# A hybrid RWKV-7 / gated DeltaNet layer on one core: the woven order set anew, and three lists of products cut differently

## The chip, the cores and the metric

The kernel runs on one core of a Trainium2 chip. A core has TensorE (PE in the profile, with its weight loads as PEld), VectorE (DVE), ScalarE (ACT), GpSimd (POOL) and SyncE (SP), which issues most DMA transfers. The metric is the device time of one execution in microseconds (us); lower is better.

## What is computed

One layer over 256 latent and 256 context tokens, model width 2048, in fp32. Cut to what matters:

```python
mod = silu(c) @ w_ada + b_ada                  # first 4096 columns: shift and scale of norm 1
h, hc = modulate(rmsnorm(x)), modulate(rmsnorm(ctx))
rw, cv, z, ab, gt = split(h @ w_in)            # the same for hc
# RWKV-7: 16 heads of 64, both directions, context states start the latent scan
s = s * w_t - (s @ kk_t) b_t + v_t k_t         # per token; run here in chunks of 64
# gated DeltaNet: 8 heads of 128, both directions, chunks of 64
lmat = strict((k * beta) @ k.T * decay)        # solved by a triangular inverse
v_new = u_i - w_i @ s                          # the first chunk's state is zero
s = s * gl_i + k_tail_i.T @ v_new              # the state after the last chunk is not read
y = (sigmoid(g_a) * (o_a @ p_a) + sigmoid(g_b) * (o_b @ p_b)) @ w_out
x = x + gt1 * y
x = x + gt2 * swiglu(modulate(rmsnorm(x)))
return rmsnorm(x)
```

The kernel handles the DeltaNet in blocks of 128 tokens: four blocks, two of context and two of latent tokens, `gorder[d]` is the order in which direction d walks over them. The state product `NW` (L1411 to L1416) belongs to blocks 2 to 4 of that order, the state update (`kta`) to blocks 1 to 3.

## The kernel before

**Matrix products.** Weights come as fp32 and are split into two parts, `whi` (rounded, by ScalarE) and `wlo` (the rest, by VectorE); three TensorE products hi x hi, hi x lo, lo x hi replace one in fp32. These are the gemm products below (`mm<-hxh,whi` and so on). All other products run in plain fp32 and show as two records each in a trace.

**Start (L422 to L546).** A matvec makes shift and scale of the first norm. It runs in eight parts (`NE`), each with 64 products `mm<-aw,ckr` of 128 columns in tiles of 32 output rows. The weights of a part come in four loads `aw` of 1 MB (`load_ada`), and two loads `w_low` (`load_low`) bring the low-rank and first head weights of the same part. `ada_part(ps, e, c)` does a quarter of a part, `low_products` gives six tiles of gemm products of the part before, and `TILES[part][c]` says how many of those tiles stand behind visit c. `rows_of` turns the result of a part and normalises its share of the tokens; tiles that are left go there.

**The woven stage (L1506 to L1526).** RWKV pairs of heads, DeltaNet heads, the input projection (`products`), its casts (`cast`), the low-rank outputs and the second matvec (`ada_rest`) are written as generators. `Weave` takes one step of one of them after another. It keeps an estimated time for each engine, starts the step that can start first, and breaks ties by `RANK` (lower first). A step that reads what another engine made is placed `LAT['hop']` later, a change of the kind of TensorE product costs `LAT['turn']`, a load costs its bytes plus `LAT['dma']`. The order that results is fixed in the program, and each engine works its own queue in that order. TensorE fills the time between the small products of a chain with gemm products.

```python
at = w[3] + (0.0 if w[4] is None else lane.own if w[4] is lane else HOP)
key = (max(self.free.get(lane, 0.0), at), w[0])
```

**What a pair of RWKV heads does.** `prepare`, then `grams` (products `pa<-LAc` and `pa<-LAl`, once a direction), then `inverse`, `values` and `scan`. `invert` writes the blocks out to memory (`scr`), reads them back as 16x16 blocks, solves those on VectorE, writes them out (`tscr`) and reads them again. Then come lists of small TensorE products with one bank of PSUM (`pib`): a first list on 32x32 tiles, a second one with `Tx`, a third and a fourth. RWKV inverts 16 blocks at a time (`nu == 16`), a DeltaNet head 8.

**Low-rank outputs (`lowrank`).** Four loads of `lora` weights (one for two pairs) go through the same SP queue as everything else; each feeds eight products `s<-lin,wraw`.

**The merge stage (from L1563)** is scheduled by the compiler's own scheduler, and some of its first instructions come to stand among the last of the woven stage: casts of `rows` to `oah`, casts of weights (L370), sigmoids of the gates (`gts`).

Of the kernel before, what the change touches and what calls it, by code (L numbers as in the profile page):

```python
# [11 lines left out]
F32 = mybir.dt.float32  # L12
F32R = mybir.dt.float32r
AF = mybir.ActivationFunctionType
# [4 lines left out]
P = 128  # L19
# [7 lines left out]
DECAY = 0.6065306597126334  # L27
GATES_A, GATES_B = (6, 2, 3, 3, 0, 1, 4, 3), (2, 2, 0, 1, 0, 2, 10, 1)

RANK = dict(cast=-94, lowrank=60, prepare=59, grams=34, inverse=-56, values=6, scan=-39, begin=196, head_scan=145, head_inverse=100, head_grams=123, decays=137, tokens=77, features=120, gate_out=137, lowrank_out=105, row_tile=486)  # L30
LAT = dict(dma=2.04, hop=0.255, own=0.092, grp=32, cg=4, turn=0.17)
LNEXP = "natural_log_exp_and_others"
SIGM = "sigmoid_and_others"
UNIT = 64 * 64 + 64
# [249 lines left out]
def emit(ctx: ExitStack, tc, A, out, dbg=None):  # L284
# [6 lines left out]
    e, v, s = Lane(E, 0.0, 0.0, 0.0), Lane(V, 0.07, 0.00104, LAT["own"], 0.13), Lane(S, 0.09, 0.00086, LAT["own"], 0.165)  # L291
# [130 lines left out]
    with tc.tile_pool(name="p0", bufs=1) as p0, \  # L422
# [12 lines left out]
        def load_ada(e, c):  # L435
            w = aws[e, c] = p0.tile([P, 4, 4, P], F32, tag="aw", name="aw", bufs=6)
            Q.dma_start(w, A["ada_first"][e, :, 4 * c:4 * c + 4])
# [16 lines left out]
        ps = pst(pa, "pa")  # L454
# [9 lines left out]
        ps = pst(pa, "pa")  # L464
# [48 lines left out]
        def low_products(e, w):  # L513

            for ps, (o, m, n) in zip(low, LOWS):
                for k in range(2):
# [1 line left out]
                         e == 0 and k == 0, e == NE - 1 and k == 1)  # L518
                yield

        TILES = ((0, 0, 0, 0), (1, 1, 1, 1), (1, 1, 1, 1), (0, 2, 1, 1), (0, 1, 2, 1),
                 (0, 2, 1, 1), (0, 1, 2, 1), (0, 1, 1, 1), (0, 2, 1, 1))
        before = None
        for part in range(NE + 1):
            if part < NE:
                ps = pst(pmm, "mm")
            for c in range(4):
                if part + 1 < NE:
                    load_ada(part + 1, c)
                if part < NE:  # L530
                    ada_part(ps, part, c)
                if c == 0 and part < NE:
                    w = low_split(part)
                    if part + 1 < NE:
                        load_low(part + 1)
                for _ in itertools.islice(before or (), TILES[part][c]):
                    pass
            if part < NE:
                rows_of(part, ps, before or ())
                before = low_products(part, w)  # L540
            else:
                for _ in before:
                    pass
# [31 lines left out]
    def invert(pool, Lt, parts, nu, which, full, fill):  # L575
# [56 lines left out]
        ps = yield pib  # L632
# [3 lines left out]
        for d in range(2):  # L636
            yield v.scalar_tensor_tensor(Qm[:, us[d]], pv[:, 0, us[d]], low16[:, d:d + 1],
                                         eye16[:, d].unsqueeze(1).to_broadcast([P, h2, 16]), ALU.mult, ALU.add)
        if nu == 16:
            yield [e.matmul(pv[64 * h:64 * h + 64, 1, u], Tx[64 * h:64 * h + 64, u, :], Qm[64 * h:64 * h + 64, u, :],  # L640
                            start=True, stop=True) for u in range(nu) for h in range(2)]
        else:
            yield [e.matmul(pv[r, 1, u], Tx[r, u, b:b + 32], Qm[r, u, :], start=True, stop=True) for h, u, b, r in fours]
        for h in range(2):
            yield [(s.copy if h else v.tensor_copy)(T0[r, us[d], b + 16 * d:b + 16 * d + 16], pv[r, 1, us[d]])
                   for d in range(2) for b in (0, 32) for r in (slice(64 * h + b, 64 * h + b + 32),)]
# [641 lines left out]
    def tokens(h):  # L1288

        o = hd[h]  # L1290
        yield "feat", h
        yield "scan", NPAIR - 1 if h else NPAIR - 2
        yield "inverse", NPAIR - 1
        if h > 1:
            yield "gscan", h - 2
        o["keg"] = keg = gs.tile([P, 2, 4, P], F32, tag="keg", name="keg")
        o["kta"] = kta = gs.tile([P, 2, 4, P], F32, tag="kta", name="kta")
        o["vt"] = vt = gs.tile([P, 4, P], F32, tag="vt", name="gvt")
        ps = yield pab
        yield [e.transpose(ps[:, P * b:P * b + P], o["v"][:, P * b:P * b + P], ident) for b in range(4)]  # L1300
        yield s.copy(vt.rearrange("p b c -> p (b c)"), ps)
        weave.release(pab)
        ps = yield pab
        yield [e.transpose(ps[:, P * b:P * b + P], o["k"][:, P * b:P * b + P], ident) for b in range(4)]
        p4 = ps.rearrange("p (b c) -> p b c", b=4)
        for d in range(2):
            col = 8 * d + h
            yield v.tensor_mul(keg[:, d], p4, egc[:, :, col:col + 1].to_broadcast([P, 4, P]))
            yield v.tensor_mul(kta[:, d], p4, eta[:, :, col:col + 1].to_broadcast([P, 4, P]))
        weave.release(pab)  # L1310
        weave.ready("tok", h)

# [87 lines left out]
    def head_scan(h):  # L1400
# [7 lines left out]
            yield "out", NPAIR - 1  # L1408
        tf, keg, kta, vt, Qe, PT = (o[n] for n in ("tf", "keg", "kta", "vt", "Qe", "PT"))

        NW = gs.tile([P, 2, 4, P], F32, tag="NW", name="NW")  # L1411
        for d in range(2):
            ps = yield psb
            yield [e.matmul(ps[:, P * b:P * b + P], keg[:, d, b, :], tf[:, 4 * d + b, :], start=True, stop=True) for b in range(4)]
            yield s.activation(NW[:, d].rearrange("p b c -> p (b c)"), ps, AF.Identity, scale=-1.0)
            weave.release(psb)  # L1416
        if h:
            yield "gout", h - 1
# [2 lines left out]
        for n in range(4):  # L1421
            bs = (gorder[0][n], gorder[1][n])
            ps = yield psb
            yield [e.matmul(ps[:, P * d:P * d + P], tf[:, 4 * d + bs[d], :], vt[:, bs[d], :], start=True, stop=n == 0) if i == 0 else
                   e.matmul(ps[:, P * d:P * d + P], NW[:, d, bs[d], :], St[:, d, :], start=False, stop=True)
                   for d in range(2) for i in range(1 + (n > 0))]
            Vn = gs.tile([P, 2, P], F32, tag="Vn", name="Vn")
            for d in range(2):
# [383 lines left out]
```

## Time and profile before

| | |
|---|---|
| median of 3 runs | 2216.26 us (2205.15 to 2219.96) |
| the profiled execution | 2212.82 us, span 2211.0 us |
| mean granted TensorE clock | 0.989 |
| TensorE busy | 2138.1 us, 97% |
| VectorE, ScalarE, GpSimd busy | 1560.2 us, 1081.2 us, 93.6 us |
| read from and written to memory | 405.76 MB, 25.84 MB |

The span reaches from the first to the last instruction; some 2 us lie around it. Line numbers in a profile are those of the kernel; where the weave issues an instruction, its line is L147, and tiles tell such groups apart. Tiles that lie in one large buffer all show as `arena`. A row like `pi<-arena,Tx 64*64 64x16` is a product into a bank `pi`, 64 rows by 64 columns of the array, with 16 columns streamed. Busy TensorE time counts products that overlap in the array once.

### The profile page before, as it was taken

What the parts mean: (1) busy time and instruction counts of PE and PEld (TensorE: products, weight loads), DVE (VectorE), ACT (ScalarE), POOL (GpSimd) and SP (SyncE); (2) the same over time, 40 slices, a digit from 0 to 9 for tenths busy, and PEclk for the clock granted to TensorE, in tenths of its full rate; (3) what the DMA queues carried; (4) which work ended last, traced back from release to release, by engine and by line L of the source; (5) the groups of instructions that cost most, each with busy time, mean ns of one, the idle gap of its engine ahead of it and who ended that gap; (6) DMA issues with size and microseconds to landing.
All of it is one profiled execution on the core that took longest, in us unless ns stands there. A gap on an engine that the chain in (4) does not pass through costs nothing. (4 is left out here: it accounts for less than half of the span.)

```text
span 2211.0 us, 54434 instructions
## 1 busy us (share of the span) xinstructions
PE 2138.1 (97%) x22780; PEld 1910.8 (86%) x22780; DVE 1560.2 (71%) x3245; ACT 1081.2 (49%) x1915; POOL 93.6 (4%) x171
## 2 busy tenths in 40 slices
PE   6998999999999999999899899999999999999998
PEld 4776678787788788887789799999999999999997
DVE  3456788888798577998998689956665655444444
ACT  3248745545456555454554465534444444444443
POOL 0000000000000010111110010100000000000000
PEclk9999899999999999999999999999999999999999
DMA  9966544444444355565567888927777776566665
GB/s 383 413 188 201 152 117 108 120 109 109 121 113 112 111 182 167 177 195 167 170 202 251 291 297 303 344 78 236 237 235 233 230 234 198 186 184 187 188 185 160
DMA packets 234486, 435.13 MB, mean 197 GB/s; under 512 B 115329, under 2 KB 129665, under 8 KB 229889
## 3 DMA queue, kind: packets, MB, share of 16 engines
q1 hardware_dynamic: 206304, 355.11, 51.1%
q0 software_dynamic: 14112, 51.39, 7.1%
q10 hardware_dynamic: 13824, 25.17, 3.4%
q8 instruction: 178, 2.92, 0.6%
q14 instruction: 68, 0.55, 0.1%
HBM read 405.76 MB, written 25.84 MB: 195 GB/s over the span
## 5 line engine op out<-in xcount | busy, mean ns | idle before, releaser
L371 DVE TENSOR_TENSOR wlo<-wraw,whi 128x1024 fp32r<-128x1024 f32 x328 | 392.7, 1198 | 319.5 <-ACT whi L370 317.4
L370 ACT CAST whi<-wraw 128x1024 fp32r<-128x1024 f32 x328 | 337.9, 1031 | 461.3 <-PE mm L381 410.6
L147 PE MATMUL mm<-hxh,wlo 128*128 128x256 f32 (+1 forms) x1376 | 460.6, 335 | 5.7 <-DVE wlo L147 5.5
L147 PE MATMUL mm<-hxh,whi 128*128 128x256 f32 (+1 forms) x1376 | 461.9, 336 | 0.9 <-ACT arena L147 0.5
L147 PE MATMUL mm<-hxl,whi 128*128 128x256 f32 (+1 forms) x1376 | 460.8, 335 | 0.0
L380 PE MATMUL mm<-hfh,whi 128*128 128x256 f32 x1344 | 376.8, 280 | 0.0
L381 PE MATMUL mm<-hfl,whi 128*128 128x256 f32 x1344 | 375.8, 280 | 0.0
L382 PE MATMUL mm<-hfh,wlo 128*128 128x256 f32 x1344 | 374.6, 279 | 0.1
L147 PEld LDWEIGHTS mm<-hxh,wlo 128*128 128x128 f32 x1376 | 260.1, 189 | 33.6 <-DVE wlo L147 8.4
L147 PEld LDWEIGHTS mm<-hxh,whi 128*128 128x128 f32 x1376 | 260.1, 189 | 27.1 <-issue 4.4
L147 PEld LDWEIGHTS mm<-hxl,whi 128*128 128x128 f32 x1376 | 260.2, 189 | 26.1 <-issue 6.2
L147 DVE TENSOR_TENSOR wlo<-wraw,whi 128x512 fp32r<-128x512 f32 x344 | 236.9, 691 | 49.5 <-ACT whi L147 48.0
L382 PEld LDWEIGHTS mm<-hfh,wlo 128*128 128x128 f32 x1344 | 252.6, 188 | 0.6 <-DVE wlo L371 0.5
L381 PEld LDWEIGHTS mm<-hfl,whi 128*128 128x128 f32 x1344 | 252.7, 188 | 0.0
L380 PEld LDWEIGHTS mm<-hfh,whi 128*128 128x128 f32 x1344 | 252.5, 188 | 0.0
L147 ACT CAST whi<-wraw 128x512 fp32r<-128x512 f32 x344 | 205.2, 616 | 96.2 <-PE mm L147 63.4
L147 DVE TENSOR_TENSOR arena<-arena 128x28 f32<-128x28 f32 (+13 forms) x538 | 132.1, 247 | 18.7 <-DMA arena<-scr 7.1
L380 PE MATMUL mm<-za,whi 128*128 128x256 f32 x512 | 144.0, 281 | 0.0
L381 PE MATMUL mm<-za,whi 128*128 128x256 f32 x512 | 143.3, 280 | 0.0
L382 PE MATMUL mm<-za,wlo 128*128 128x256 f32 x512 | 142.4, 278 | 0.0
L147 ACT ACTIVATE arena<-arena 128x512 f32<-128x512 f32 (+3 forms) x132 | 76.8, 592 | 40.1 <-DVE arena L147 37.3
L381 PEld LDWEIGHTS mm<-za,whi 128*128 128x128 f32 x512 | 96.3, 188 | 0.0
(329 smaller groups left out, 3911.3 us busy)
## 6 DMA issues: line engine op xcount, KB each, us to landing
wraw<-w SPq DMA_DIRECT2D x172, 512.0 KB, 4.3
wraw<-wgu SPq DMA_DIRECT2D x168, 512.0 KB, 4.7
aw<-ada_rest POOLq DMA_DIRECT2D x96, 512.0 KB, 5.5
aw<-ada_first SPq DMA_DIRECT2D x32, 1024.0 KB, 12.6
wraw<-wdn SPq DMA_DIRECT2D x64, 448.0 KB, 3.6
wraw<-wout SPq DMA_DIRECT2D x32, 512.0 KB, 6.3
aw<-ada_gt ACTq DMA_DIRECT2D x64, 256.0 KB, 4.9
wraw<-wdn SPq DMA_DIRECT2D x32, 512.0 KB, 3.6
```

What stands on the lines that cost most here:

```text
L147: return Op(self, cost, lambda: getattr(self.engine, name)(out, *a, **k), kind)
L370: S.copy(hi[:, c, :M], raw[:, c, :M])
L371: V.tensor_sub(lo[:, c, :M], raw[:, c, :M], hi[:, c, :M].bitcast(F32))
L380: E.matmul(ps, hi, Xh[:, k, :n], start=first and i == 0, stop=False)
L381: E.matmul(ps, hi, Xl[:, k, :n], start=False, stop=False)
L382: E.matmul(ps, lo, Xh[:, k, :n], start=False, stop=last and i == len(wt) - 1)
```

## The change

It has four parts.

- `RANK` and two of the estimates in `LAT` get other numbers: a hand-over between engines (`hop`) 0.2167 instead of 0.255 us, a change of kind (`turn`) 0.1819 instead of 0.17.
- The start takes two quarters of a part in one visit, and their loads are issued together.
- With 16 blocks, `invert` builds its second list from 64 products on 32x32 tiles, as it does with 8 blocks; before it had 32 products on 64x64 tiles.
- `NW` has three blocks a direction instead of four, without the first of the order; in the second direction `keg` of the first block and `kta` of the last are not made either.

```diff
-RANK = dict(cast=-94, lowrank=60, prepare=59, grams=34, inverse=-56, values=6, scan=-39, begin=196, head_scan=145, head_inverse=100, head_grams=123, decays=137, tokens=77, features=120, gate_out=137, lowrank_out=105, row_tile=486)
-LAT = dict(dma=2.04, hop=0.255, own=0.092, grp=32, cg=4, turn=0.17)
+RANK = dict(cast=-94, lowrank=43, prepare=59, grams=36, inverse=-56, values=6, scan=-66, begin=196, head_scan=150, head_inverse=132, head_grams=123, decays=125, tokens=77, features=120, gate_out=97, lowrank_out=105, row_tile=486)
+LAT = dict(dma=2.04, hop=0.2167, own=0.092, grp=32, cg=4, turn=0.1819)
...
-        TILES = ((0, 0, 0, 0), (1, 1, 1, 1), (1, 1, 1, 1), (0, 2, 1, 1), (0, 1, 2, 1),
-                 (0, 2, 1, 1), (0, 1, 2, 1), (0, 1, 1, 1), (0, 2, 1, 1))
+        TILES = ((0, 0), (2, 2), (2, 2), (2, 2), (1, 3), (2, 2), (1, 3), (1, 2), (2, 2))
         before = None
         for part in range(NE + 1):
             if part < NE:
                 ps = pst(pmm, "mm")
-            for c in range(4):
+            for c in range(2):
                 if part + 1 < NE:
-                    load_ada(part + 1, c)
+                    for i in (2 * c, 2 * c + 1):
+                        load_ada(part + 1, i)
                 if part < NE:
-                    ada_part(ps, part, c)
+                    for i in (2 * c, 2 * c + 1):
+                        ada_part(ps, part, i)
                 if c == 0 and part < NE:
                     w = low_split(part)
                     if part + 1 < NE:
...
         for d in range(2):
             yield v.scalar_tensor_tensor(Qm[:, us[d]], pv[:, 0, us[d]], low16[:, d:d + 1],
                                          eye16[:, d].unsqueeze(1).to_broadcast([P, h2, 16]), ALU.mult, ALU.add)
-        if nu == 16:
-            yield [e.matmul(pv[64 * h:64 * h + 64, 1, u], Tx[64 * h:64 * h + 64, u, :], Qm[64 * h:64 * h + 64, u, :],
-                            start=True, stop=True) for u in range(nu) for h in range(2)]
-        else:
-            yield [e.matmul(pv[r, 1, u], Tx[r, u, b:b + 32], Qm[r, u, :], start=True, stop=True) for h, u, b, r in fours]
+        yield [e.matmul(pv[r, 1, u], Tx[r, u, b:b + 32], Qm[r, u, :], start=True, stop=True) for h, u, b, r in fours]
         for h in range(2):
             yield [(s.copy if h else v.tensor_copy)(T0[r, us[d], b + 16 * d:b + 16 * d + 16], pv[r, 1, us[d]])
                    for d in range(2) for b in (0, 32) for r in (slice(64 * h + b, 64 * h + b + 32),)]
...
         p4 = ps.rearrange("p (b c) -> p b c", b=4)
         for d in range(2):
             col = 8 * d + h
-            yield v.tensor_mul(keg[:, d], p4, egc[:, :, col:col + 1].to_broadcast([P, 4, P]))
-            yield v.tensor_mul(kta[:, d], p4, eta[:, :, col:col + 1].to_broadcast([P, 4, P]))
+            late, soon = (slice(0, 4 - d), slice(d, 4))
+            yield v.tensor_mul(keg[:, d, late], p4[:, late], egc[:, late, col:col + 1].to_broadcast([P, 4 - d, P]))
+            yield v.tensor_mul(kta[:, d, soon], p4[:, soon], eta[:, soon, col:col + 1].to_broadcast([P, 4 - d, P]))
         weave.release(pab)
         weave.ready("tok", h)
 
...
             yield "out", NPAIR - 1
         tf, keg, kta, vt, Qe, PT = (o[n] for n in ("tf", "keg", "kta", "vt", "Qe", "PT"))
 
-        NW = gs.tile([P, 2, 4, P], F32, tag="NW", name="NW")
+        NW = gs.tile([P, 2, 3, P], F32, tag="NW", name="NW")
         for d in range(2):
             ps = yield psb
-            yield [e.matmul(ps[:, P * b:P * b + P], keg[:, d, b, :], tf[:, 4 * d + b, :], start=True, stop=True) for b in range(4)]
-            yield s.activation(NW[:, d].rearrange("p b c -> p (b c)"), ps, AF.Identity, scale=-1.0)
+            yield [e.matmul(ps[:, P * i:P * i + P], keg[:, d, b, :], tf[:, 4 * d + b, :], start=True, stop=True)
+                   for i, b in enumerate(gorder[d][1:])]
+            yield s.activation(NW[:, d].rearrange("p b c -> p (b c)"), ps[:, :3 * P], AF.Identity, scale=-1.0)
             weave.release(psb)
         if h:
             yield "gout", h - 1
...
             bs = (gorder[0][n], gorder[1][n])
             ps = yield psb
             yield [e.matmul(ps[:, P * d:P * d + P], tf[:, 4 * d + bs[d], :], vt[:, bs[d], :], start=True, stop=n == 0) if i == 0 else
-                   e.matmul(ps[:, P * d:P * d + P], NW[:, d, bs[d], :], St[:, d, :], start=False, stop=True)
+                   e.matmul(ps[:, P * d:P * d + P], NW[:, d, n - 1, :], St[:, d, :], start=False, stop=True)
                    for d in range(2) for i in range(1 + (n > 0))]
             Vn = gs.tile([P, 2, P], F32, tag="Vn", name="Vn")
             for d in range(2):
```

Where the order of the program changes, at three places. First TensorE in the start, part 1 of the matvec (a piece of the difference; `aw,ckr` are the matvec's products, `C,rows` turns part 0, `hxh,whi` and `hxl,whi` begin the first low-rank tile).

```order
 L483 MATMUL pa<-C,rows 128x128
-L475 MATMUL mm<-aw,ckr 32x128 x16
+L475 MATMUL mm<-aw,ckr 32x128 x32
 L380 MATMUL pi<-hxh,whi 128x512
 L381 MATMUL pi<-hxl,whi 128x512
```

A visit that had a quarter of the part now has half of it. Over the whole start TensorE goes to the matvec 15 times instead of 24.

Second the queue of SyncE around the first inversion and the fourth load of low-rank weights, before and then now (`scr` is the list being written and read, `tscr` the solved blocks, `w` weights of the input projection, `sgd` low-rank outputs read back, `gts` a stored gate).

```order
L169 DMA scr_105<-arena 64x8x64 x3
L169 DMA wraw<-w 128x1024 x2
L169 DMA scr_105<-arena 64x8x64
L169 DMA arena<-sgd__1347 128x512
L169 DMA wraw<-lora 96x1024
L169 DMA arena<-scr_105 128x16x16
L169 DMA wraw<-w 128x1024 x2
```

```order
L169 DMA wraw<-w 128x1024 x2
L169 DMA scr_105<-arena 64x8x64 x3
L1062 DMA gts__1356<-arena 128x256
L169 DMA wraw<-w 128x1024
L169 DMA scr_105<-arena 64x8x64
L169 DMA arena<-sgd__1347 128x512
L169 DMA wraw<-lora 96x1024
L169 DMA arena<-scr_105 128x16x16
L169 DMA wraw<-w 128x1024 x2
```

The load of `lora` still stands behind the fourth piece of `scr` and one of `sgd`. Between the third and the fourth piece there is now one load of `w` and a stored gate where two loads of `w` were. On TensorE there stand, between the second product list `pa<-LAl` of the first pair and the first product with that load, 39 gemm products of 256 columns, two low-rank products and a list of four transposes before; now 50 of 256 columns, one of 512, two low-rank products and two lists of four transposes. Between that product and the first list of the inversion there were 34 of 512 and 9 of 256 columns, now 47 and 42, beside the other seven low-rank products; a list of four transposes that stood there stands ahead now.

Third the queue of ScalarE at the end of the woven stage, before and then now (`T_...` and `Tx` are copies of the last head's inversion, `TF_...` its result, L370, L385 and L1594 or L1593 belong to the merge stage).

```order
L147 COPY T_15211<-pi 32x4x16 x4
L370 CAST whi<-wraw 128x1024 x2
L147 COPY arena<-mm 128x256
L385 CAST oah<-arena 128x512 x4
L147 COPY Tx<-pi 32x4x32 x2
L1594 ACT_TABLE_LOAD
L1594 ACTIVATE gts<-gts 128x512 x2
L147 COPY T_15211<-pi 32x4x32 x2
L147 COPY TF_10119<-Tx 64x8x64 x2
```

```order
L147 COPY Tx<-pi 32x4x32 x2
L147 COPY arena<-mm 128x256
L147 CAST whi<-wraw 128x512
L147 COPY T_15395<-pi 32x4x32 x2
L147 COPY TF_10310<-Tx 64x8x64 x2
L147 CAST whi<-wraw 128x512
L370 CAST whi<-wraw 128x1024
L147 COPY TF_10310<-pi 64x4x64 x2
L147 ACTIVATE arena<-s 128x384
L370 CAST whi<-wraw 128x1024
L147 COPY arena<-mm 128x256
L385 CAST oah<-arena 128x512 x4
```

The cast of `oah`, which stood ahead of the copies to `Tx`, now stands behind the result, and the sigmoids of `gts` follow it. VectorE's queue moves in the same way: two splits of merge weights (L371) and four of `oal` (L386) stood among the copies of that inversion and now come behind them.

## The prediction

> **What bounds the kernel now.** The page comes first: how busy is each engine, and where does the busiest of them stop.
>
> ```profile
> span 2211.0 us, 54434 instructions
> PE 2138.1 (97%) x22780; PEld 1910.8 (86%) x22780; DVE 1560.2 (71%) x3245; ACT 1081.2 (49%) x1915; POOL 93.6 (4%) x171
> ```
>
> TensorE (PE) is busy for 97% of the span, so at most 73 us of its idle time can be given back; anything more has to be work that PE no longer does. Next the stages, to see where those 73 us lie.
>
> ```profile
> 200.00:250.00 50.00, 39.27 (x329) 25.58 (x327) 27.95 (x72) 38.63 (x72) 1.45 (x4) 0.83 0.60 173
> 250.00:300.00 50.00, 49.31 (x739) 40.20 (x735) 42.85 (x91) 28.69 (x67) 1.59 (x6) 1.00 0.44 127
> 1200.00:1250.00 50.00, 44.20 (x545) 41.98 (x545) 39.84 (x104) 21.24 (x43) 3.95 (x7) 0.93 0.72 236
> 1500.00:1550.00 50.00, 50.00 (x431) 50.00 (x431) 30.88 (x47) 21.42 (x29) 0.00 (x0) 1.00 0.72 231
> ```
>
> The columns are stretch, length, then busy time and number of instructions of PE, its weight loads, VectorE (DVE), ScalarE (ACT), GpSimd, and last the granted clock, DMA share and GB/s. From 1500 us on PE is simply full, and the change touches nothing there. The woven stage (about 130 to 1260 us) is nearly full too, as the slice from 250 shows, but two slices are not: 200 to 250 loses 10.7 us and runs at a mean clock of 0.83, 1200 to 1250 loses 5.8. The waits name the largest cause.
>
> ```profile
> PE s L147 <- DMA wraw<-lora: 8.1, 2, 7.1
> PE s L147 <- ACT VX L147: 0.4, 1, 0.4
> ```
>
> One transfer, the fourth load of the low-rank weights, costs the most. So PE's own work counts everywhere in the woven stage, and order counts in a few places.
>
> **1. The inversion's list: less PE work.** The trace shows both forms of list, one behind the other, in the first inversion.
>
> ```profile
> 248.78 1.26 PE L147 MATMUL pi<-arena 32*32 32x16 f32 x128
> 249.97 0.50 PE L147 MATMUL mm<-hxl,whi 128*128 128x512 f32 x1
> 251.56 2.04 PE L147 MATMUL pi<-arena,Tx 64*64 64x16 f32 x64
> 253.53 0.51 PE L147 MATMUL mm<-hxl,whi 128*128 128x512 f32 x1
> ```
>
> The 32x32 list (64 products, two records each in fp32) takes PE from 248.78 to 249.97, 1.19 us; the 64x64 list (32 products) from 251.56 to 253.53, 1.97 us. The changed list has the shape, count and places of the first. It saves 0.78 us, in eight inversions 6.2 us. PE is full there, so all of it should reach the end; between 0 (if VectorE, busy 42.85 of 50 us, takes over as the bound) and 6.2 I take 6.2, since PE's 49.31 is nearer to full. [...]
>
> **2. Unread head products: less PE work.**
>
> ```profile
> 865.03 0.28 PE L147 MATMUL mm<-hxh,wlo 128*128 128x256 f32 x1
> 865.15 1.05 PE L147 MATMUL s<-TF,keg 128*128 128x128 f32 x8
> 865.96 0.36 PE L147 MATMUL mm<-hxh,whi 128*128 128x256 f32 x1
> ```
>
> Four products of keg hold PE from 865.15 to 865.96, 0.20 us each. Two per head and eight heads go: 16 x 0.20 = 3.2 us. The two shorter multiplications on VectorE and the two shorter copies on ScalarE per head lie beside PE work and count as nothing; were that cover gone, they would give a few microseconds more, never less.
>
> **3. The first matvec in two visits: hidden by DMA.**
>
> ```profile
> 97.64 1.95 PE L475 MATMUL mm<-aw,ckr 128*32 128x128 f32 x64
> 99.52 0.51 PE L380 MATMUL pi<-hxh,whi 128*128 128x512 f32 x1
> 105.09 1.08 PE L475 MATMUL mm<-aw,ckr 128*32 128x128 f32 x32
> 106.10 0.48 PE L380 MATMUL s<-hxh,whi 128*96 128x512 f32 x1
> 106.42 0.40 PE L381 MATMUL s<-hxl,whi 128*96 128x512 f32 x1
> 106.65 0.39 PE L382 MATMUL s<-hxh,wlo 128*96 128x512 f32 x1
> 109.91 1.96 PE L475 MATMUL mm<-aw,ckr 128*32 128x128 f32 x64
> ```
>
> A visit of 16 products lasts 1.01 us (105.09 to 106.10), one of 32 lasts 1.88 (97.64 to 99.52), and the first gemm product behind a visit starts its successor 0.32 instead of 0.23 later (106.10, 106.42, 106.65). A merged pair saves 2 x 1.01 - 1.88 + 0.09, about 0.23 us, plus some 0.09 of switching in; the order has 24 visits before and 15 after, so 9 x 0.32 = 2.9 us at most. But one part lasts 109.91 - 97.64 = 12.27 us, and its loads need nearly as long.
>
> ```profile
> DMA packets 6688, 37.76 MB, mean 410 GB/s; under 512 B 740, under 2 KB 779, under 8 KB 2827
> aw<-ada_first SPq DMA_DIRECT2D x27, 1024.0 KB, 12.4
> wraw<-w_low SPq DMA_DIRECT2D x13, 368.0 KB, 10.2
> ```
>
> Four loads of 1024 KB and two of 368 KB are 4.95 MB, at 410 GB/s 12.07 us. DMA is therefore 0.2 us per part behind PE, and the saving cannot shorten a part by more. At the end it even turns round: the visit that needs the last load now has 32 products instead of 16 (+0.9 us) and one low-rank tile more behind it (six products of 0.23, +1.4 us). I take 0.5 us of gain, between 2.9 and a loss of 2.3.
>
> **4. The order around the fourth low-rank load.**
>
> ```profile
> 207.76 1.10 PE L147 MATMUL pa<-LAl,arena 64*64 64x128 f32 x32
> 216.44 0.28 PE L147 MATMUL mm<-hxh,wlo 128*128 128x256 f32 x1
> 223.78 2.08 PE L147 MATMUL s<-lin,wraw 96*128 96x512 f32 x2 [7.06 <-DMA wraw<-lora]
> 230.20 3.78 PE L147 MATMUL s<-lin,wraw 96*128 96x512 f32 x4 [1.57 <-ACT lo L147]
> ...
> 220.00:235.00 15.00, 9.65 (x22) 5.93 (x23) 8.07 (x29) 10.91 (x22) 0.00 (x0) 0.50 0.53 147
> ...
> 212.08 1.75 SPq L169 DMA_DIRECT2D wraw<-w  x2
> 213.93 0.58 SPq L169 DMA_DIRECT2D scr<-arena  x1
> 215.27 1.01 SPq L169 DMA_DIRECT2D wraw<-lora  x1
> 222.36 0.38 SPq L169 DMA_DIRECT2D arena<-scr  x1
> ```
>
> The inversion's list is written out (scr), then the load is issued behind it in the same queue at 215.27 and lands at 223.78; PE waits 7.06 us, then 1.57 more, and runs at half clock until about 237. The 15 us from 220 hold 9.65 us of PE work at a clock of 0.50, so half of it, about 5 us, is lost as well: some 14 us in all. The round trip is what lasts: from the second product of grams (207.76) to the first list (248.78) 41.0 us. The change leaves the load behind the list in the queue, but with one weight load of 512 KB between them instead of two (1.3 us at the 410 GB/s of part 3). And the new order puts more PE work into the same 41 us. Ahead of the waiting product: 11 more products of 256 columns (0.117 each, see the 0.12 from 865.03 to 865.15), one of 512 (0.23) and four transposes (0.4, at the 0.10 a record of part 2), together 1.9 us. Between it and the first list: 47 products of 512 columns instead of 34 and 42 of 256 instead of 9, without four transposes that stood there, 6.5 us. So 8.4 us of work move into a hole that stays about as long; the wait for the load itself should shrink from 7.06 by 1.9 and 1.3 to some 4 us. I take 8 us, between 0 (the half clock and the wait stay whole) and 14 (both go). [...]
>
> **5. The end of the weave.**
>
> ```profile
> PE pi L147 <- ACT T L147: 2.3, 1, 2.3
> PE pi L147 <- DVE qo L147: 2.1, 1, 2.1
> PE pi L147 <- ACT Tx L147: 1.3, 1, 1.3
> ...
> 1245.00:1250.00 5.00, 3.68 (x47) 3.61 (x47) 4.95 (x10) 2.51 (x5) 0.29 (x1) 0.50 1.04 365
> ...
> L385 ACT CAST oah<-arena 128x512 fp32r<-128x512 f32 x8 | 4.7, 620 | 1.8 <-PE mm L382 1.5
> ```
>
> The last head's inversion here stands behind the merge stage's casts and gate sigmoids on ScalarE and VectorE, and PE waits 5.7 us for its copies, with another 1.8 us lost to half clock (half of 3.68). In the new order those copies stand ahead of that work. What comes late next is the cast of the merge's input, now behind the last gate copy; PE has the heads' products there, some 2 us, against a cast of 0.62 us (the last row) and a subtraction that I estimate at the same, with their hand-overs. I take 5 us, between 7.5 and a loss of 1.
>
> **6. Shorter hand-overs: the cost.** The estimate of a hand-over falls from 0.255 to 0.217, so consumers are placed sooner. In the scans' steps the work between the product and the one that needs its copy drops by about one product of 256 columns (0.117 us), in some 120 places. The wait for VX above is 0.4 us in all, so these links fit today; by how much is not shown. Bounds: 0 and 120 x 0.117 = 14 us; I take 3, nearer to the row.
>
> ```profile
> 735.00:740.00 5.00, 5.00 (x17) 4.32 (x17) 1.63 (x3) 1.72 (x9) 0.00 (x0) 0.50 0.02 6
> ```
>
> In this stretch PE is busy throughout and the clock is halved all the same, which costs about half of the 5.00 us. The new order may be rid of it; I count nothing.
>
> **Sum.** -6.2 - 3.2 - 0.5 - 8 - 5 + 3 = -19.9 us. Against the profiled execution's own 2212.82 us that is 2193; the median of the runs, 2216.26, lies 3.4 above that execution, so on its footing 2196. I say 2194. One per cent (22 us) is about what a measurement of this kernel can tell from no change.
>
> **Rivals.** *The holes move.* PE's order is fixed by a plan that underrates this DMA round trip in both versions; wait and half clock at the fourth load could stay whole, and the end give 2 instead of 5. Then -6.2 - 3.2 - 0.5 - 2 + 3, about 2204. For it: the load still follows the list in the queue. Against: 8.4 us of work that were not there before. 23%.
>
> [...] 20%.
>
> *The links become the bound, and it is slower.* If the tighter hand-overs fall short everywhere they are used, the 120 scan links and about as many in the heads' inversions and scans each wait 0.15 us: 36 us against the 20 gained, 2229. It decides once a link falls short by about 0.09 us, since 240 x 0.09 is all of the gain. Against it: the waits for VX are small today. 7%.
>
> My own case has 50%, with 2187 to 2201 for itself. The range 2176 to 2212 takes in the first two rivals and leaves out the last. Below 2194 lies half of my case and the second rival: faster by over 1% 0.46; within 1% 0.49; slower by over 1% 0.05.
>
> **What would show it.** Right: the 32x32 list eight more times at 1.19 us and no 64x64x16 group; PE's wait for the load under 5 us; no waits for T, Tx and qo at the end; the matvec's last visit still ending near 118 us. Wrong: a wait for the load as long as now, half-clock slices in new places, or the waits of s for ACT VX and DVE grown to several microseconds. The forecast fails most easily if the round trip of part 4 grows, since everything behind the first inversion hangs on it.

## The result, and the profile after

The change made the kernel slower by about 1%: 2235.72 us median (2234.44 to 2238.0) against 2215.38, a ratio of 1.0097 (95% interval 1.0068 to 1.0126). A second set of runs, beside other runs of the kernel before, gave 1.0105 (1.0088 to 1.0121). The forecast was 2194 us, with 2176 to 2212 as the range. The page of the changed kernel:

```profile
span 2234.7 us, 55415 instructions
PE 2139.9 (96%) x23260; PEld 1912.7 (86%) x23260; DVE 1559.2 (70%) x3245; ACT 1076.3 (48%) x1915; POOL 94.4 (4%) x171
```

PE's busy time is nearly what it was (2138.1), but its idle time, span less busy, went from 72.9 to 94.8 us. The stages show where. The columns are those of the prediction: stretch, length, then busy time and instructions of PE, its weight loads, VectorE, ScalarE and GpSimd, the granted clock, DMA share and GB/s. First the kernel before:

```profile
0.00:200.00 200.00, 178.88 (x1786) 130.93 (x1787) 102.33 (x246) 90.48 (x165) 1.37 (x8) 0.98 0.85 308
200.00:300.00 100.00, 88.57 (x1063) 65.79 (x1061) 70.80 (x163) 67.31 (x138) 3.04 (x10) 0.91 0.52 150
300.00:800.00 500.00, 495.60 (x7277) 398.50 (x7277) 408.79 (x1032) 266.09 (x616) 19.46 (x43) 0.99 0.41 114
800.00:1200.00 400.00, 387.11 (x4115) 334.96 (x4114) 360.79 (x923) 206.20 (x406) 45.03 (x68) 1.00 0.62 191
1200.00:1350.00 150.00, 140.90 (x1374) 136.64 (x1374) 119.35 (x229) 79.11 (x123) 12.68 (x23) 0.98 0.83 288
```

Then the changed kernel:

```profile
0.00:200.00 200.00, 171.35 (x1730) 125.84 (x1731) 97.10 (x236) 88.01 (x159) 1.37 (x8) 0.97 0.83 303
200.00:300.00 100.00, 92.41 (x1123) 71.36 (x1121) 75.24 (x168) 70.41 (x145) 3.76 (x10) 0.93 0.58 161
300.00:800.00 500.00, 480.47 (x7642) 385.01 (x7642) 391.59 (x1000) 249.99 (x592) 16.94 (x38) 0.98 0.39 107
800.00:1200.00 400.00, 385.86 (x3800) 330.70 (x3799) 350.39 (x904) 204.15 (x401) 43.88 (x66) 0.99 0.59 179
1200.00:1350.00 150.00, 140.27 (x1576) 133.74 (x1575) 124.20 (x249) 79.02 (x137) 16.39 (x30) 0.99 0.87 304
```

Idle time of PE is the length less the first busy time. From 200 to 300 us, where the forecast placed its largest gain, it falls from 11.4 to 7.6 us and the clock rises from 0.91 to 0.93. From 300 to 800 us, where the kernel before stops for 4.4 us in half a millisecond and the forecast looked only at list lengths and links, it rises to 19.5 us and the clock falls from 0.99 to 0.98. Up to 200 us there are 7.5 us more. The two kernels are not at the same work at the same time, so two common marks help: the last product of the input projection starts at 1242.84 us before and at 1271.19 now, the first product of swiglu at 1451.76 and 1479.43. The woven stage begins 0.9 us later than before, so the loss arises within it, and none behind the first mark. The waits name what stands there now:

```profile
PE pi L147 <- issue: 10.2, 6, 3.0
PE mm L147 <- DVE wlo L147: 6.4, 4, 3.9
PE s L147 <- DMA wraw<-lora: 6.2, 3, 3.0
PE mm L475 <- DMA aw<-ada_first: 6.1, 7, 1.5
PE mm L382 <- DVE wlo L371: 4.1, 4, 2.2
PE pa L147 <- issue: 2.5, 2, 2.3
PE mm L380 <- ACT whi L370: 2.2, 2, 1.6
```

The first row is new. It is the inversion's second list, and "issue" means that PE waits for nothing that the profile shows. In order of time, at the second inversion:

```profile
329.98 1.26 PE L147 MATMUL pi<-arena 32*32 32x16 f32 x128
331.17 0.44 PE L147 MATMUL pa<-C,arena 128*128 128x128 f32 x2
...
332.70 1.08 PE L147 MATMUL pi<-arena,Tx 32*32 32x16 f32 x107
336.76 0.51 PE L147 MATMUL pi<-arena,Tx 32*32 32x16 f32 x21 [2.98 <-issue]
337.20 1.99 PE L147 MATMUL pa<-LAl,arena 64*64 64x128 f32 x32
```

Two lists of 128 records start within 3 us (329.98 and 332.70); the second stops after 107 of them, for 2.98 us, in the middle of a list whose inputs are all there. Stops of this kind (1.39, 0.74, 1.81, 1.86, 1.47 us) stand in five more of the eight, and one of 2.34 us in the products of KB behind the last. In a second execution of the changed kernel (e13) the six lists stop after exactly the same records (107, 58, 78, 114, 65 and 120). A 5 us stretch behind the first of them:

```profile
335.00:340.00 5.00, 3.24 (x55) 2.77 (x55) 1.90 (x6) 1.03 (x4) 0.00 (x0) 0.56 0.03 5
```

The clock is halved in most of it as well (mean 0.56).

### The profile page after: what moved, and what is told of

It reads as the page before. It is cut to its first block, busy times and chain, and to the rows that moved or that the text cites. A ratio compares the mean times of both kernels' runs of the same rounds, so it can differ in the third digit from the quotient of the medians.

```text
span 2234.7 us, 55415 instructions
## 1 busy us (share of the span) xinstructions
PE 2139.9 (96%) x23260; PEld 1912.7 (86%) x23260; DVE 1559.2 (70%) x3245; ACT 1076.3 (48%) x1915; POOL 94.4 (4%) x171
## 3 DMA queue, kind: packets, MB, share of 16 engines
q8 instruction: 182, 2.98, 0.6%
## 4 chain that ended last, share of the span: by engine, by line
issue 38%; PE 35%; DVE 15%; DMA 8%; ACT 3%; SPq 1%; POOL 0%; ACTq 0%; POOLq 0%; DVEq 0%
PE mm L147 17%; DVE arena L147 5%; PE s L147 4%; PE pa L147 4%; DVE wlo L147 3%; PE mm L382 2%; PE mm L381 2%; PE mm L380 2%; PE pi L147 2%; DMA aw<-ada_first 2%; DVE aw L147 2%; DMA arena<-tscr 1%; ACT lo L147 1%; DMA wraw<-lora 1%; DMA wraw<-w_low 1%
## 5 line engine op out<-in xcount | busy, mean ns | idle before, releaser
L371 DVE TENSOR_TENSOR wlo<-wraw,whi 128x1024 fp32r<-128x1024 f32 x328 | 392.9, 1199 | 317.8 <-ACT whi L370 314.8
L370 ACT CAST whi<-wraw 128x1024 fp32r<-128x1024 f32 x328 | 337.2, 1029 | 460.8 <-PE mm L381 396.7
L147 PE MATMUL mm<-hxh,wlo 128*128 128x256 f32 (+1 forms) x1376 | 464.5, 338 | 6.6 <-DVE wlo L147 6.4
L147 PE MATMUL mm<-hxh,whi 128*128 128x256 f32 (+1 forms) x1376 | 467.3, 340 | 3.5 <-ACT arena L147 1.8
L147 PE MATMUL mm<-hxl,whi 128*128 128x256 f32 (+1 forms) x1376 | 466.1, 339 | 0.0
L147 PEld LDWEIGHTS mm<-hxh,wlo 128*128 128x128 f32 x1376 | 263.8, 192 | 34.0 <-DVE wlo L147 7.7
L147 PEld LDWEIGHTS mm<-hxh,whi 128*128 128x128 f32 x1376 | 263.7, 192 | 31.4 <-issue 5.7
L147 PEld LDWEIGHTS mm<-hxl,whi 128*128 128x128 f32 x1376 | 264.0, 192 | 26.1 <-issue 4.9
L147 DVE TENSOR_TENSOR wlo<-wraw,whi 128x512 fp32r<-128x512 f32 x344 | 236.9, 690 | 56.9 <-ACT whi L147 55.7
L147 ACT CAST whi<-wraw 128x512 fp32r<-128x512 f32 x344 | 204.4, 616 | 81.8 <-PE mm L147 44.7
L147 DVE TENSOR_TENSOR arena<-arena 128x28 f32<-128x28 f32 (+13 forms) x538 | 130.9, 248 | 15.5 <-DMA arena<-scr 3.4
L147 ACT ACTIVATE arena<-arena 128x512 f32<-128x512 f32 (+3 forms) x132 | 77.2, 592 | 56.7 <-DVE arena L147 53.8
```

The costliest lines, as they stand in the source:

```text
L147: return Op(self, cost, lambda: getattr(self.engine, name)(out, *a, **k), kind)
L370: S.copy(hi[:, c, :M], raw[:, c, :M])
L371: V.tensor_sub(lo[:, c, :M], raw[:, c, :M], hi[:, c, :M].bitcast(F32))
```

## The experiments

Three theories were tried. *Theory 1, instruction supply*: PE's instructions themselves come by DMA, and two lists of 64 small products in a row use them up faster than they arrive. The page lists such transfers:

```profile
q8 instruction: 182, 2.98, 0.6%
```

182 packets of 2.98 MB are 16 KB each. PE's 23260 products and as many weight loads are 46520 instructions, 256 for each packet: the queue is PE's (178 packets for 45560 such instructions in the kernel before, 183 for 46840 in e8), and a list of 128 records with their weight loads is one packet. *Theory 2*: the stops come from the new order, or from small tiles. *Theory 3*: any new plan loses, whatever it was made from, because the order of before happens to avoid stops that other orders meet. Each ratio below is against runs of the kernel before on the same chip.

**The supply by itself (e8).**

```diff
-        yield [e.matmul(pv[r, 0, u], ...) for h, u, b, r in fours]
+        for _ in range(6 if weave.lists == 1 else 1):
+            yield [e.matmul(pv[r, 0, u], ...) for h, u, b, r in fours]
```

> The kernel before with the first inversion's first list of 64 products (32x32 tiles, 256 instructions with their weight loads) issued six times in a row; the repeats write the same values. It measures the supply of instructions by itself. Theory 1: the first one or two lists run at 1.2 us, the others at the pace at which blocks of 16 KB arrive, 3 to 5 us each, so the six last 15 to 22 us with stops that the profile calls 'issue'. Theory 2 (small products need no supply): six lists in 7.2 us without a stop.

One run, 2266.5 us; the planner counted the repeats and laid out a new order behind them, so only the lists themselves are read here. PE at the six lists, in order of time:

```profile
249.31 2.44 PE L147 MATMUL pi<-arena 32*32 32x16 f32 x270
255.46 1.90 PE L147 MATMUL pi<-arena 32*32 32x16 f32 x128 [3.70 <-issue]
259.73 1.91 PE L147 MATMUL pi<-arena 32*32 32x16 f32 x128 [2.37 <-issue]
263.73 1.90 PE L147 MATMUL pi<-arena 32*32 32x16 f32 x128 [2.10 <-issue]
267.46 1.73 PE L147 MATMUL pi<-arena 32*32 32x16 f32 x114 [1.82 <-issue]
```

PE gets through 270 records, 540 instructions with their weight loads, and from then on through exactly 128 at a time, one packet's worth, at 4.27, 4.00 and 3.73 us from start to start. The six lists take 19.9 us instead of 7.2. The trace's packet records show the supply itself: packets of that queue end at 253.98, 258.29, 262.32 and 266.23 us, and PE goes on 1.2 to 1.5 us behind each (in the changed kernel one ends at 335.24, and the list that stopped goes on at 336.76). No two packets of this queue start within 3.3 us of each other in either trace. Theory 1 holds: PE gets through some two packets' worth without a stop here (540 instructions, 2.1 times 256), a list that uses up one packet lasts 1.26 us at full clock, and the next packet takes 3.7 to 4.3. The 270 records that run without a stop are small products too, so small tiles by themselves did not stop PE here.

**The list undone in the new order (e1 and, beside the changed kernel again, e14 and e13).** The plan still counts 64 small products, so every other instruction of the changed kernel keeps its place.

```diff
-        yield [e.matmul(pv[r, 1, u], ...) for h, u, b, r in fours]
+        small = [e.matmul(pv[r, 1, u], ...) for h, u, b, r in fours]
+        yield planned_as(small, [32 products on 64x64 tiles]) if nu == 16 else small
```

> The changed kernel with one thing undone: the inversion's second list is again 32 products on 64x64 tiles; the plan still counts it as 64 small ones, so every other instruction keeps its place. Theory 1 (instruction supply): TensorE's instructions come by DMA in blocks (182 packets, 2.98 MB on the instruction queue, 16 KB each); two lists of 64 small products within 3 us use up more blocks than come in, so the list stops in the middle (2.98, 1.39, 0.74, 1.81, 1.86, 1.47 us 'issue', and 2.34 us in the products of KB behind the last) and the clock halves behind most stops. Then these 12.5 us of 'issue' waits and some 10 us of half clock go, the list itself costs 6.2 more: about 2219 us (2212 to 2225). Theory 2 (order): the stops come from the new order, for instance instructions of other engines that the profile does not show as waits; then the waits stay before the same list and it is 6 us slower, about 2242.

> The changed kernel as it is, to stand beside the next one on the same chip: about 2236 us, with some 10 us of waits called 'issue' in the second lists.

> The changed kernel with the second list on 64x64 tiles again and every other instruction in its place, a second time: its first profile showed 13 us less than the changed kernel's, its timed runs none. Theory 1 (the 32x32 list loses more by its stops than its 7 us): 5 to 15 us faster than the changed kernel beside it. Rival (in this order the stops cost about what the list saves): within 5 us of it.

```profile
PE pi L147 <- issue: 1.1, 2, 0.7
```

That is e1; then e13 and e14:

```profile
PE pi L147 <- issue: 10.5, 6, 3.2
PE pi L147 <- issue: 3.4, 4, 1.7
```

VectorE, ScalarE and SyncE work in the same order in the traces of the changed kernel, e1 and e14. The stops went, mostly, as theory 1 says: 10.2 to 1.1 us, 10.5 to 3.4 the second time. The time did not follow: 2236.3 us (1.0092, 1.0060 to 1.0125), though the one profiled execution took 2223. The second time, 2234.4 (1.0086, 1.0068 to 1.0104) beside 2238.5 for the changed kernel (1.0105). So in this order the 32x32 list loses some 1 to 4 us, and the intervals overlap: its stops and the half clock behind them about eat up the 6 us of work that it was to save. The expectation of 2219 was wrong, since the list is not what makes the changed kernel slow.

**The list alone in the old order (e2).** The same helper, the other way round.

> The kernel before with the second list alone on 32x32 tiles (planned at the price of the 64x64 one, so that the order of the woven stage stays). Theory 1 (instruction supply): stops of 0.7 to 3 us in the middle of most of the eight second lists, half clock behind several: 10 to 20 us slower than before, about 2230. Theory 2 (order): no stops, the list takes 1.2 instead of 2.0 us eight times: 6 us faster, about 2209.

2244.6 us, 1.0135 (1.0102 to 1.0168): slower by 30, where theory 1 asked for 10 to 20.

```profile
PE pi L147 <- issue: 10.8, 9, 2.8
PE pa L147 <- issue: 2.9, 1, 2.9
PE mm L147 <- issue: 2.0, 2, 1.2
```

15.7 us of "issue" where the kernel before has 0.2, and a mean clock of 0.980 instead of 0.989. The stops come in the old order too, so the new order does not make them; with the 270 records of e8, theory 2 falls. But not all of the 30 us are the list's. The woven stage kept its order; the merge stage, which the compiler schedules, did not (VectorE's splits of merge weights and its products PA come in another order). The profiled execution, 39 us behind that of the kernel before, is 21.6 us behind at the last product of the input projection (1264.43 against 1242.84) and 39.4 at the first of swiglu (1491.20 against 1451.76). What the list cost where the order was held is therefore about 22 us of that execution, near theory 1; the other 18 go with a merge stage that came out differently.

**More room between the lists (e3).**

```diff
+        if nu == 16:
+            yield 2.5
         yield [e.matmul(pv[r, 1, u], ...) for h, u, b, r in fours]
```

> The changed kernel with both lists on 32x32 tiles, but the plan holds the second list back by 2.5 us, so that more gemm products stand between the two lists (15 instead of 8 in the first inversion that shows a stop). Theory 1 (instruction supply): a block has time to arrive, 'issue' waits in the second lists fall from 10.2 to under 3 us in all, the second list takes 1.3 us each and the half clock behind it goes; the inversion's chain grows by 2.5 us, which PE covers with gemm work: about 2216 us (2208 to 2226). Theory 2 (order, or the small tiles themselves): the stops stay as long, 2236 or more.

2236.3 us, 1.0102 (1.0073 to 1.0132). The waits for "issue" in the lists fell from 10.2 to 3.8 us, so room between lists does feed PE; the time stayed, with 7.2 us of waits of the inversion for VectorE's copies (4.6 in the changed kernel) and other losses in a plan that was new throughout. The time of e3 is therefore no measure of the gap alone.

**The order alone (e4), and its two halves (e6: LAT, e7: RANK).**

```diff
-RANK = dict(cast=-94, lowrank=60, ...)
-LAT = dict(dma=2.04, hop=0.255, own=0.092, grp=32, cg=4, turn=0.17)
+RANK = dict(cast=-94, lowrank=43, ...)
+LAT = dict(dma=2.04, hop=0.2167, own=0.092, grp=32, cg=4, turn=0.1819)
```

> The kernel before with the new RANK and LAT alone (second list on 64x64 tiles, head products and matvec as before). By the prediction's terms 4 to 6 the order alone gives 8 + 5 - 3 = 10 us: about 2205. By the trace of the change it gives nothing or loses: the load's wait shrinks (8.1 to 6.2 us in all) but new waits for the casts of weights stand at 254 to 256 us (3.4 us, with 10 us of half clock behind) and at 1171 and 1276 to 1311 us: about 2215 to 2224.

> The kernel before with the two new estimates of LAT alone (hand-over 0.2167, change of kind 0.1819). If the shorter hand-over is what makes the new order slow (the prediction's term 6, bounded there by 0 and 14 us): about 2240, most of the 34 us of ranks and estimates together. If the ranks are: within 8 us of before. Theory 3: 2225 to 2240 here and for the ranks alone as well.

> The kernel before with the new RANK alone. If the ranks make the new order slow (work moved into the first inversion whose weight splits then stand behind a waiting instruction): about 2240, with waits for wlo behind the DMA of the solved blocks near 255 us. If the estimates are: within 8 us of before. Theory 3: 2225 to 2240 here and for the estimates alone as well.

e4: 2247.1 us, 1.0157 (1.0122 to 1.0192), worse than either expectation. e6: 2231.1, 1.0074 (1.0046 to 1.0103). e7: 2246.6, 1.0151 (1.0120 to 1.0182). Both halves lose, LAT by what theory 3 expected of it, RANK by more. The stage from 300 to 800 us of e4:

```profile
300.00:800.00 500.00, 486.95 (x7183) 392.00 (x7184) 395.99 (x1004) 256.20 (x601) 15.13 (x38) 0.99 0.41 112
```

13.1 us idle where the kernel before has 4.4, and all second lists in this stretch are on 64x64 tiles.

**A null edit (e11).**

```diff
-LAT = dict(dma=2.04, hop=0.255, own=0.092, grp=32, cg=4, turn=0.17)
+LAT = dict(dma=2.04, hop=0.254, own=0.092, grp=32, cg=4, turn=0.17)
```

> The kernel before with a null edit: the estimate of a hand-over 0.254 instead of 0.255. It changes no work and no estimate by more than half a per cent, but ties fall another way and some 4000 of 36000 lines of the order differ. Theory 3: this plan loses like the others, 10 to 30 us, 2224 to 2244. Rival (the new ranks and estimates are worse, plans as such are alike): within 5 us of before.

2257.4 us, 1.0204 (1.0181 to 1.0228): slower by some 40 us, twice what the change lost, by an edit that means nothing.

```profile
200.00:300.00 100.00, 85.56 (x1001) 64.62 (x1000) 65.25 (x151) 62.40 (x128) 3.01 (x10) 0.88 0.46 137
300.00:800.00 500.00, 485.99 (x7150) 393.21 (x7149) 393.46 (x997) 256.54 (x600) 13.82 (x37) 0.98 0.42 114
800.00:1200.00 400.00, 377.74 (x3776) 318.58 (x3775) 344.51 (x887) 201.15 (x390) 44.85 (x67) 0.98 0.55 170
1200.00:1350.00 150.00, 138.19 (x1544) 132.74 (x1543) 111.22 (x247) 78.07 (x137) 12.16 (x22) 0.95 0.77 259
```

14.4, 14.0, 22.3 and 11.8 us idle, against 11.4, 4.4, 12.9 and 9.1; the clock is lower in every stage. Every new plan that was run has lost, as theory 3 says; that any other would is not shown.

**The small parts, with a plan of their own (e5) and in the old order (e9).**

```diff
-            yield v.tensor_mul(keg[:, d], p4, ...)
+            old = v.tensor_mul(keg[:, d], p4, ...).cost
+            yield priced(old, v.tensor_mul(keg[:, d, late], p4[:, late], ...))
...
+            four[3].call = lambda: None
+            yield four
```

> The kernel before with the two small parts of the change alone: unread head products left out and the matvec in two visits a part; RANK, LAT and the 64x64 list as before (a plan of its own, since the head products are fewer). By the prediction's terms 2 and 3: -3.2 and -0.5, about 2209 us against 2213. If the parts simply add up, the runs so far ask for more: the order alone cost 34 us and order with these two parts 23, so -11, about 2202. If instead any new plan loses what the old one had (theory 3: the plan before happens to miss the stops and halvings that other plans meet), 2215 to 2235, with more idle time and half clock in the woven stage and less work in full-clock time.

> The two small parts of the change (unread head products left out, matvec in two visits) with the order of the kernel before held fixed: the plan still counts the work that is left out, so apart from the start every instruction keeps its place. Theory 3 (a new plan loses by itself): the 13 us that the same two parts lost with a plan of their own go, and the work that is gone shows: terms 2 and 3 of the prediction, -3.7, about 2210 us (2205 to 2213). Rival (the parts themselves lose, for instance by shorter cover or by the matvec's waits): about 2227 again.

The same work is left out in both, and the matvec is the same. e5: 2227.5 us, 1.0054 (1.0029 to 1.0079), 12 us slower. e9: 2212.1 us beside 2216.9 for the kernel before, 0.999 (0.9974 to 1.0006). Two stages of e9:

```profile
200.00:300.00 100.00, 88.21 (x1087) 65.95 (x1086) 70.72 (x163) 68.04 (x142) 3.03 (x10) 0.95 0.52 151
300.00:800.00 500.00, 495.60 (x7265) 398.55 (x7260) 409.88 (x1034) 264.91 (x614) 18.85 (x43) 0.99 0.41 114
```

From 300 to 800 us PE is busy for 495.60 us, as in the kernel before (that the hundredths agree is chance), and the last product of the input projection starts at the same time, 1242.8 us. Work that goes under an order that stays costs nothing and may give a few microseconds; the same cut with a new plan loses 12. (The merge stage keeps its order in e9 but for a few instructions.) e9 is the best version that was run, and it is not told apart from the kernel before.

The runs in one table. Idle is span less PE's busy time; the next column, one less the mean clock, times the span, bounds what half clock took; the last is busy time less that.

| kernel | ratio | span | idle | half clock, at most | work at full clock |
|---|---|---|---|---|---|
| before | 1 | 2211.0 | 72.9 | 24.3 | 2113.8 |
| changed | 1.0097 | 2234.7 | 94.8 | 35.8 | 2104.1 |
| e1, list undone | 1.0092 | 2221.4 | 84.9 | 26.7 | 2109.8 |
| e2, list alone, old order | 1.0135 | 2250.3 | 100.0 | 45.0 | 2105.3 |
| e3, room between the lists | 1.0102 | 2247.1 | 94.8 | 42.7 | 2109.6 |
| e4, order alone | 1.0157 | 2241.5 | 85.9 | 38.1 | 2117.5 |
| e5, small parts, own plan | 1.0054 | 2231.9 | 92.7 | 33.5 | 2105.7 |
| e6, LAT alone | 1.0074 | 2227.8 | 87.6 | 31.2 | 2109.0 |
| e7, RANK alone | 1.0151 | 2244.7 | 93.7 | 42.6 | 2108.4 |
| e9, small parts, old order | 0.9990 | 2207.8 | 76.6 | 30.9 | 2100.3 |
| e11, null edit | 1.0204 | 2265.5 | 103.5 | 49.8 | 2112.2 |
| e13, changed again | 1.0105 | 2239.5 | 95.9 | 35.8 | 2107.8 |
| e14, list undone again | 1.0086 | 2237.6 | 90.6 | 38.0 | 2109.0 |

Spans are of one profiled execution each, and these differ by some 10 us within a kernel. The last column should agree for before, e4, e6, e7 and e11, which do the same work; it differs by 9, so it shows no difference under that.

The idle time does not grow at one kind of wait. The woven stage's `pi` products, which are the inversions', wait 9.5 us for other engines and DMA in the kernel before and 7.3 in the changed one, but 26.7 in e11, 19.3 in e5 and 17.3 in e7; in e4 the projection's products wait longer for split weights (`PE mm L147 <- DVE wlo L147` 11.2 us instead of 5.5); in the changed kernel the waits for "issue" grow most, from 0.2 to 12.7 us, nearly all of them in the lists. Nor does all of it stand in the woven stage: between the last product of the input projection and the first of swiglu, the profiled executions of e5, e7 and e11 take 9 to 11 us longer than the kernel before, those of e4, e6 and the changed kernel do not.

## Why the prediction was wrong

1. **The list.** Its length was right: 128 records in 1.26 us again in the one list that neither stops nor runs at half clock (748.17 us; 1.90 at half clock). "All of it should reach the end" was wrong, and so were the bounds of 0 to 6.2: in the old order the list lost about 22 us of a profiled execution where the order was held (e2), in the new one some 1 to 4. The step asked whether VectorE could become the bound, and never whether PE would get its instructions; the row of q8 stood on the page, and the list doubles the instructions from 128 to 256 within 1.2 us.
2. **Unread head products.** Right.

```profile
L147 PE MATMUL s<-TF,keg 128*128 128x128 f32 x96 | 13.3, 274 | 0.0
```

96 records in 13.3 us, where there were 128 in 16.9: 3.6 us for the forecast's 3.2, and in an order held fixed (e9) they cost nothing elsewhere.

3. **The matvec.** Its mechanism was right. Its last visit of 32 products is the last two rows here, cut in two by the wait for its load:

```profile
109.94 1.96 PE L475 MATMUL mm<-aw,ckr 128*32 128x128 f32 x64
113.41 1.08 PE L475 MATMUL mm<-aw,ckr 128*32 128x128 f32 x32
115.54 1.08 PE L475 MATMUL mm<-aw,ckr 128*32 128x128 f32 x32 [1.05 <-DMA aw<-ada_first]
```

The last 16 start at 115.54 instead of 116.00, the forecast's 0.5 us, and PE waits 6.1 us for these loads in all instead of 2.5: the saving went into waits for DMA, as worked out. The gain does not reach the woven stage, which begins 0.9 us later than before (0.4 in e13).

4. **The fourth load.** Mostly right in its place, too large in its size. The waits for such loads fell from 8.1 to 6.2 us in all, the longest from 7.1 to 3.0 (7.3 and 4.6 in the second execution, e13). Behind that longest wait, the 2.96 us ahead of 226.34, the clock is halved all the same, from 226.39 to 229.81 us by the trace's clock records; the 14 us for wait and half clock together, which the second rival, given 20%, needed here, are shown by no run. But the round trip did not stay at about 41 us, on which the step rests: from the second product of grams to the first list it takes 44.1 us (212.75 to 256.86), 47.0 in e13. It opened again behind the load. PE, then VectorE:

```profile
253.88 0.39 PE L147 MATMUL mm<-hxh,whi 128*128 128x256 f32 x1 [1.60 <-ACT whi L147]
256.19 0.39 PE L147 MATMUL mm<-hxh,wlo 128*128 128x256 f32 x1 [1.80 <-DVE wlo L147]
```

```profile
249.66 0.47 DVE L147 SCALAR_TENSOR_TENSOR arena<-mm,mq,arena 128x252 f32<-128x252 f32 x1
254.46 0.71 DVE L147 STREAM_TRANSPOSE Tx<-arena 128x512 f32<-128x512 f32 x1 [4.32 <-DMA arena<-tscr]
255.09 0.44 DVE L147 SCALAR_TENSOR_TENSOR arena<-mm,mq,arena 128x252 f32<-128x252 f32 x1
255.45 0.68 DVE L147 TENSOR_TENSOR wlo<-wraw,whi 128x512 fp32r<-128x512 f32 x1
```

The work that was moved into the round trip needs split weights (wlo); its split at 255.45 stands in VectorE's queue behind a transpose that waits 4.32 us for the solved blocks. With these 3.4 us of waits for whi and wlo and a halved clock from 257 to 267, the stretch from 200 to 300 us gained 3.8 us of idle time and at most 2 of clock, about 6 for the forecast's 8. In e13 the same stretch has 8.8 us of idle time and a clock of 0.90: 2.6 gained and up to 1 lost. The step failed where it counted PE's work as cover without asking whose queue feeds that work. (That the head-of-queue wait is the cause is read from the rows; no run took it away.)

5. **The end of the weave.** The waits for T, qo and Tx went nearly as forecast: from 1150 to 1350 us they were 5.7 us before and are 0.4 now. What came late next was said to be one cast; it was the merge stage's operands, in the same stretch 3.0 us for wlo (L371), 2.2 for whi (L370) and 1.7 for oal (L386), where the kernel before waits 0.2 for wlo and 1.0 for oah. Idle time from 1200 to 1350 us rose from 9.1 to 9.7, though all of this lies 28 us later, so the stretch does not match exactly.

6. **Shorter hand-overs.** The forecast's 0 to 14 us looked at scan links alone. LAT alone cost 16 us (e6), and not in those links: idle time before the products of VX with C and with KB is 2.7 us in e6 and 2.0 in the changed kernel, against 1.0 before.

What failed beyond sizes is the sum itself. It went through the places where the old order stops, counted each as closing in part, and let all others stand as they were. But the planner lays out the whole woven stage anew for any number that changes, the compiler the merge stage behind it, and six new plans of the old kernel or parts of it (e4, e5, e6, e7, e11, and the changed kernel's own) had 13 to 31 us more idle time than the kernel before, whatever they were made from. None was faster. The rival "the holes move" named the mechanism, but priced it only at the holes that were there, at 2204; for a slowdown of this size there was one mechanism, the links, and it was given 7%. Why the old plan stops so little is not shown, nor whether its numbers had been found by trying many; the runs show only that the new plans tried here all stop more, one of them for a change of 0.001 in one estimate.

## What to carry to other kernels

Where a planner sets the order, an edit of one number or price draws a whole new order, and the profile of the old one says little about the new: hold the order fixed to learn what an edit of the work is worth, and treat each new plan as a draw of its own, whose spread a null edit shows. A product that gets shorter by being cut into more instructions has a second price, the supply of instructions; count them per microsecond against the packets of the instruction queue (here 256 in 1.26 us, against a packet of 256 every 3.7 to 4.3 us in e8). An order is held only where the traces say so: here one edit (e2) left the planner's stage as it was and still changed the stage behind it. Work moved into a wait is cover only if the engine that prepares it is not itself queued behind that wait (here the split at 255.45 us, behind a transpose that waited 4.32 us).

## What the runs showed of the hardware

PE's supply of instructions, in e8: some 540 in hand, then 256 per 3.7 to 4.3 us. Its half clock: the granted clock in all fourteen traces changes only on a fixed raster of 3.41 us. Cut on that raster between 100 and 1450 us, of 93 windows at full clock with at least 1.8 us of PE idle time in them, 91 were followed by half clock; of 5071 with less than 1.0 us, 12 were, and of 146 in between, 30 (worked out from the clock records and PE's rows of all traces). Those 12 all hold a list of small products, ten of them the 64x64 one with 16 columns: PE is busy there by the profile, and the clock is halved behind it as behind a stop, which is what stood unexplained at 735 us in the prediction. Most such lists have no such effect: of 67 windows with that 64x64 list in them and as little idle time, these 10 were followed by half clock. An estimate from these counts: a stop of 2 us may cost another 1.7 us, half of a window of 3.41 us, or nothing, by where the raster falls; that this is a reason why executions of one kernel differ by 10 us is likely, but not shown.
